# Row maxima of attention logits: two heads in the two halves of TensorE's rows instead of one head at a time

## Chip, cores and metric

The kernel runs on one core of a Trainium2 chip. The metric is the device time of one execution in microseconds (us). The core's engines are TensorE (PE in the profile; its weight loads are PEld), VectorE (DVE), ScalarE (ACT), GpSimd (POOL) and SyncE (SP), which here only issues transfers. Each engine works through its own instructions in order and waits on semaphores that others raise.

## The reference

One layer of a streaming encoder over 4096 tokens of width 1024. The part that matters is the sparse attention with 8 query heads of 64 in two groups, each group sharing one key and value head:

```python
iscore = jnp.where(allowed[None], iscore, -jnp.inf)
_, idx = lax.top_k(iscore, k_sel)                 # 256 keys for each query
...
s = jnp.einsum('bqgrd,bqkgd->bqgrk', qg, kg).astype(jnp.float32) * scale
s = jnp.where(valid[:, :, None, None, :], s, -jnp.inf)
p = jax.nn.softmax(s, axis=-1).astype(v.dtype)
o = jnp.einsum('bqgrk,bqkgd->bqgrd', p, vg)
```

Around it stand an RMS norm, the input projection, the index scores that choose the keys, a pooling branch, gates and the output projection. A softmax doesn't change when the same number is taken off all logits of a row, so the maximum that is subtracted may be a rough one.

## The kernel before

The kernel has four stages in a row: projection, index scores with the choice of keys, attention, output. Attention is the one that the change touches. It is dense: all keys up to the query's block are used, and a bias of 0 or -1e30 from the choice of keys takes out the others.

Queries are cut into 32 blocks `b` of 128. A unit is one block and one group `g` of four heads, so there are 64 units, and a unit of block `b` has `b + 1` tiles of 128 keys (1056 in all). For precision every number is held as a high part and a low part. `kk` holds the high part of the keys in rows 0 to 63 and again in rows 64 to 127, `kl` the low part in rows 0 to 63; `qa` holds the high parts of the queries in rows 0 to 63 and their low parts in rows 64 to 127, `qm` the high parts in rows 0 to 63 and, in row 64, the row's maximum.

For each unit:
- `maxima` (L1263): for each of the four heads, and for each chunk of up to 1024 keys, TensorE multiplies the head's 128 queries in `qa` with `kk` (L1280, up to two matmuls of 512 columns) into a tile `ps` of two banks, of which there are two. VectorE adds the bias and takes the maximum in one instruction (L1286), and at the end one maximum over the chunks (L1292). The maxima go through memory (`maxD`) into row 64 of `qm`.
- `softmax` (L1299): for each key tile TensorE makes the logits of four heads, keys in rows and queries in columns, with two matmuls (L1319, L1320) into one of three tiles `st` of one bank; VectorE adds the turned bias `bT` (L1323) into `tt`; ScalarE takes the exponential (L1326); GpSimd adds the exponentials up in `acc` (L1350, two key tiles at once); TensorE multiplies them with the values into `pv` (L1335), for up to four key tiles in one go, two heads into the lower 64 output partitions and two into the upper 64, each with 64 columns of weights. At the end the sums over keys are taken with a matmul (L1371), in the same split of columns.
- `queries` (L1217) turns the queries of a block by TensorE transposes (L341) through `st`, and ScalarE copies them into `qa` and `qm` (L1245, L1246).

The order of each engine's instructions is not that of the code. `Plan` (L120) plays all steps through with a cost in us, a due time (`key`) and tiles that must be free, and records them as they start: at each moment a free engine takes the step with the earliest key whose inputs are there and whose tiles are free. A change of `form` between two steps of an engine adds `CHF` (0.12) to the cost. What the chip does with that fixed order is another matter.

Of the kernel before, what the change touches and what calls it, by code (L numbers as in the profile page):

```python
# [12 lines left out]
F32 = mybir.dt.float32  # L13
F32R = mybir.dt.float32r
# [52 lines left out]
WOK = 45.0  # L67
WOD = 0.0
PVN = 4
IVL = 12.0  # L70
DU = 4
RB = 2
# [47 lines left out]
class Plan:  # L120
# [11 lines left out]
    def new(self, name):  # L132
        return Tile_(name)
# [113 lines left out]
class K:  # L247
# [893 lines left out]
    def phase_attention(self):  # L1141
# [26 lines left out]
        esr = ExitStack()  # L1168
        rp = esr.enter_context(tc.tile_pool(name="br", reuse_waits="tile", bufs=1, side="right"))
        shapes = {"k4": (K4, [P, 2, 2, 192], F32R), "q2": (2, [P, 8, P], F32R), "bias": (BB, [P, S], BF),  # L1170
                  "jk": (JK, [P, 1024], BF), "qa": (QB, [P, 8, P], F32R), "qm": (QB, [65, 8, P], F32R),
                  "bT": (2, [P, NB, P], BF), "mx": (4, [P, 4, 4], F32), "mf": (4, [P, 4], F32),
                  "tt": (TB, [P, 2, 4, P], F32), "acc": (2, [P, 2, 4, P], F32), "ov": (OV, [P, 2, P], F32),
                  "sm": (1, [P, 2, P], F32), "rl": (2, [P, 32], F32)}
        last = {"qa": (NB - 1) % QB, "qm": (NB - 1) % QB, "bT": (NB - 1) % 2}
        early = ("k4", "q2", "bias", "jk", "mf", "mx")
        banks = {"st": (SB, [P, 4, P], F32), "ps": (2, [P, 1024], F32), "pv": (1, [P, 2, P], F32)}
        pl = Plan()
        new = pl.new
        for pool, rings in ((sp, shapes), (pp, banks)):  # L1180
# [36 lines left out]
        def queries(b, base):  # L1217

            rows = slice(b * P, (b + 1) * P)
            L = P * (b + 1)  # L1220
            bias, q2, qa, qm = new("bias"), new("q2"), new("qa"), new("qm")
            ld = pl.add("dma", 0.8, base - 8, lambda: sp_dma(
                q2.t.rearrange("p h c -> p (h c)").bitcast(F32), self.hlD[rows, H_Q:H_K]), use=[q2])

            def load_bias():
                if b < 2:
                    gp.memset(bias.t[:, :L], 0.0)
                    gp.memset(bias.t[0:64, L - 64:L], -1e30)
                else:
                    sp_dma(bias.t[:, :L], self.biasD[b, :, :L])  # L1230
            lb = pl.add("pool" if b < 2 else "dma", 0.3 if b < 2 else 0.8, base - 8, load_bias, last_lb, use=[bias])
            last_lb[:] = [lb]
            done = []
            for f in range(2):
                pt = new("st")
                key = base + 2 + f
                sl = slice(f * 4, f * 4 + 4)

                def turn(pt=pt, f=f):
                    for h in range(4):  # L1240
                        self.turn(pt.t[:, h], q2.t[:, 4 * f + h])
                t = pl.add("pe", 0.24, key, turn, [ld], use=[pt, q2, qa, qm])

                def put(pt=pt, sl=sl):
                    act.activation(qa.t[:, sl], pt.t, AF.Copy)  # L1245
                    act.activation(qm.t[0:64, sl], pt.t[0:64], AF.Copy)  # L1246
                done.append(pl.add("act", 1.0, key, put, [t], use=[pt, qa, qm]))
            BI[b], Q[b] = (bias, lb), (qa, qm, done)

        def flip(b):  # L1250

# [11 lines left out]
        def maxima(u):  # L1263
# [4 lines left out]
            base, span = (at[u - 1], at[u] - at[u - 1]) if u else (-1, 1)  # L1268
            mx, mf = new("mx"), new("mf")
            last = None  # L1270
            for j in range(4):
                for c in range(n_c):
                    o, n = c * 1024, min(1024, L - c * 1024)
                    key = base + span * (j * L + o) / (4 * L) - AL
                    ps = new("ps")

                    def mm(ps=ps, o=o, n=n, j=j):
                        for s in range(0, n, 512):
                            e = min(n, s + 512)
                            pe.matmul(ps.t[:, s:e], Q[b][0].t[:, 4 * g + j], kk[:, g, o + s:o + e], start=True, stop=True)  # L1280
                    m = pl.add("pe", 0.44e-3 * n, key, mm, Q[b][2] + [K_[k] for k in range(o // P, (o + n) // P)], [ps],
                               [Q[b][0]])
                    jk = new("jk")

                    def reduce(ps=ps, jk=jk, o=o, n=n, c=c, j=j):
                        v.tensor_tensor_reduce(out=jk.t[:, :n], in0=ps.t[:, :n], in1=BI[b][0].t[:, o:o + n], scale=1.0,  # L1286
                                               scalar=-3e38, op0=OP.add, op1=OP.max, accum_out=mx.t[:, j, c:c + 1])
                    first = last is None
                    last = pl.add("dve", 0.075 + 1.04e-3 * n, key, reduce, [m, last, BI[b][1]],
                                  [jk] + ([mx] if first else []), [ps, BI[b][0]] + ([] if first else [mx]))  # L1290
            key = at[u] - AL + 0.5
            last = pl.add("dve", 0.12, key, lambda: v.tensor_reduce(  # L1292
                out=mf.t, in_=mx.t[:, :, 0:n_c], op=OP.max, axis=AX.X), [last], [mf], [mx])
# [5 lines left out]
        def softmax(u):  # L1299
            b, g = units[u]  # L1300
            hs = slice(4 * g, 4 * g + 4)
            qa, qm, _ = Q[b]
            bt, turned = BT[b]
            acc, pv, prev, pvs, T, E, done = new("acc"), new("pv"), None, None, {}, {}, 0
            direct = DIR if u == len(units) - 1 else 0
# [127 lines left out]
        for i in range(2):  # L1433
# [1 line left out]
            s0 = pl.add("dma", 1.0, E0 - 45, lambda g=g, i=i: sp_dma(  # L1435
                g.t, self.gD[8 + 2 * i:10 + 2 * i, :, 0:w2].rearrange("k p c -> p k c")), [s], use=[g])
            for m in (2 * i, 2 * i + 1):
                ps = new("ps")

                def mm(ps=ps, m=m):  # L1440
                    ms = slice(m * P, (m + 1) * P)
                    for k in range(4):
                        for x, y in ((0, 0), (0, 1), (1, 0)):
                            pe.matmul(ps.t[:, :w2], self.wb.get(x, k, ms), xs[k // 2][y].t[:, k % 2],
                                      start=(k == x == y == 0), stop=(k == 3 and x == 1))
# [199 lines left out]
```

## Time and profile before

| | us |
|---|---|
| runs of the kernel | 4258.36, 4262.97, 4265.87; median 4262.97 |
| the profiled execution | 4264.02, span 4262.3 |
| TensorE busy in the span (matmuls) | 4137.7 (97%) |
| VectorE, ScalarE, GpSimd busy | 3217.1 (75%), 2344.9 (55%), 1903.4 (45%) |

The busy shares are means over four stages. The rows of the section below are from views of the same execution: busy time by stretch, who waited for whom, a timeline of single engines (rows of the same line that follow each other are merged, with their count), and groups of instructions by line. In a timeline a row's second number is the time from the start of its first instruction to the end of its last. Matmuls are pipelined: the next begins while the one before has not ended, so the step from start to start is what one costs.

### The profile page before, as it was taken

To read this page: it belongs to the slowest core of one execution; us is meant where nothing else is said; L and a number is where in the kernel's file an instruction comes from. 1 tells how busy PE (TensorE), PEld (TensorE's weight loads), DVE (VectorE), ACT (ScalarE), POOL (GpSimd) and SP (SyncE) were. 2 spreads that over 40 slices of the span, in tenths; PEclk is the share of its full clock that TensorE was granted. 3 is DMA by queue.
4 is the path that set the end of the run, shared out by engine and by line. 5 is a ranking of instruction groups with operands and counts; after the bars stand their busy time and mean duration, and the time that the engine had idled before them with its cause. 6 is when DMAs were issued, how large, how long until landed. Compare 5 with 4: busy or idle time off the path is not lost.

```text
span 4262.3 us, 76690 instructions
## 1 busy us (share of the span) xinstructions
PE 4137.7 (97%) x27746; PEld 3492.4 (82%) x27747; DVE 3217.1 (75%) x7786; ACT 2344.9 (55%) x3977; POOL 1903.4 (45%) x1717
## 2 busy tenths in 40 slices
PE   8999899999999999999799999999999999999999
PEld 7988799899999998999756666666666658999998
DVE  5554688889899888788679999999999995434342
ACT  5444588767877877887455555555555552111110
POOL 3455222323234333010047888888999991111110
PEclk9999999999999999999899999999999999999999
DMA  6666644545444446565543212212111016544442
GB/s 227 242 239 233 208 156 169 176 172 184 166 174 164 163 168 196 204 233 200 190 85 72 57 45 49 48 47 52 42 41 39 23 42 190 163 134 151 137 144 77
DMA packets 442041, 586.32 MB, mean 138 GB/s; under 512 B 148861, under 2 KB 337849, under 8 KB 437434
## 3 DMA queue, kind: packets, MB, share of 16 engines
q1 hardware_dynamic: 441658, 581.39, 42.0%
q8 instruction: 219, 3.59, 0.3%
q14 instruction: 164, 1.34, 0.1%
HBM read 388.54 MB, written 175.54 MB: 132 GB/s over the span
## 4 chain that ended last, share of the span: by engine, by line
PE 47%; DVE 1%; DMA 1%; POOL 1%; issue 0%; ACT 0%; SPq 0%; DVEq 0%; POOLq 0%; ACTq 0%
PE pv L1335 11%; PE st L1319 7%; PE ps L1280 6%; PE st L1320 6%; PE po L1533 3%; PE po L1534 3%; PE po L1535 3%; PE pa L1534 3%; PE pa L1535 3%; PE pa L1533 3%; PE st L1371 1%; PE st L341 1%; POOL acc L1350 0%; DVE tt L1323 0%; DMA maxD<-mf 0%
## 5 line engine op out<-in xcount | busy, mean ns | idle before, releaser
L1052 PE MATMUL pd<-h,wgh 128*128 128x256 f32 x3584 | 1017.7, 284 | 1.3 <-DVE zsm L972 1.3
L1053 PE MATMUL pd<-h,wgh 128*128 128x256 f32 x3584 | 1011.1, 282 | 0.0
L1054 PE MATMUL pd<-h,wgl 128*128 128x256 f32 x3584 | 1010.5, 282 | 0.0
L1350 POOL TENSOR_TENSOR acc<-acc,tt 128x1024 f32<-128x1024 f32 x388 | 928.6, 2393 | 100.4 <-ACT tt L1326 77.4
L1326 ACT ACTIVATE tt<-tt 128x512 f32<-128x512 f32 x1056 | 653.7, 632 | 554.6 <-DVE tt L1323 552.7
L1323 DVE TENSOR_TENSOR tt<-st,bT 128x512 f32<-128x512 f32 x1056 | 694.4, 686 | 74.9 <-PE st L1320 57.8
L770 DVE SCALAR_TENSOR_TENSOR ring<-rl,wi,ring 128x1024 f32<-128x1024 f32 (+7 forms) x624 | 692.1, 1153 | 12.9 <-ACT rl L768 10.3
L1052 PEld LDWEIGHTS pd<-h,wgh 128*128 128x128 f32 x3584 | 679.7, 190 | 19.7 <-issue 1.5
L1053 PEld LDWEIGHTS pd<-h,wgh 128*128 128x128 f32 x3584 | 680.4, 190 | 14.7
L1286 DVE CUSTOM_DVE_ANT_0 jk<-ps,bias 128x1024 bf16<-128x1024 f32 (+7 forms) x640 | 657.2, 1030 | 44.3 <-PE ps L1280 34.4
L1054 PEld LDWEIGHTS pd<-h,wgl 128*128 128x128 f32 x3584 | 680.3, 190 | 0.0
L768 ACT ACTIVATE rl<-ps 128x1024 f32<-128x1024 f32 (+7 forms) x624 | 539.5, 890 | 134.5 <-PE ps L765 61.9
L1335 PE MATMUL pv<-tt,vv 128*64 128x256 f32 x4224 | 525.2, 389 | 0.0
L855 ACT ACTIVATE sg<-ring,tk 128x2048 fp8e4<-128x2048 f32 (+7 forms) x322 | 486.0, 1511 | 37.8 <-DVE tk L842 21.7
L1319 PE MATMUL st<-qa,kk 128*128 128x512 f32 x1056 | 452.1, 428 | 9.7 <-DVE tt L1323 5.5
L1335 PEld LDWEIGHTS pv<-tt,vv 128*64 128x64 f32 x4224 | 279.6, 137 | 210.7 <-issue 72.4
L1320 PE MATMUL st<-qm,kl 65*128 65x512 f32 x1056 | 419.9, 398 | 3.5 <-DMA qm<-maxD 3.5
L1575 POOL TENSOR_TENSOR ga<-ga,gb 128x256 f32<-128x256 f32 x128 | 100.8, 797 | 618.7 <-DVE ga L1570 507.3
L1280 PE MATMUL ps<-kk,qa 128*128 128x512 f32 (+3 forms) x1152 | 361.9, 390 | 0.7 <-DVE mx L1286 0.7
L765 PE MATMUL ps<-kis,qT 128*128 128x512 f32 (+3 forms) x1136 | 336.3, 383 | 14.4 <-ACT rl L768 14.3
L1498 ACT ACTIVATE yh<-ga 128x256 fp32r<-128x256 f32 x128 | 53.5, 419 | 501.7 <-PE po L1534 297.5
L1319 PEld LDWEIGHTS st<-qa,kk 128*128 128x128 f32 x1056 | 199.8, 189 | 151.4 <-DVE tt L1323 47.5
(329 smaller groups left out, 7792.5 us busy)
## 6 DMA issues: line engine op xcount, KB each, us to landing
h<-hD SPq DMA_DIRECT2D x192, 1024.0 KB
hlD<-rhl SPq DMA_DIRECT2D x32, 1280.0 KB
gD<-sgm SPq DMA_DIRECT2D x256, 128.0 KB
x<-x SPq DMA_DIRECT2D x32, 512.0 KB
wraw<-w_in SPq DMA_DIRECT2D x32, 512.0 KB
hD<-hh SPq DMA_DIRECT2D x32, 512.0 KB
hD<-hl SPq DMA_DIRECT2D x32, 512.0 KB
q<-hlD SPq DMA_DIRECT2D x32, 512.0 KB
```

The costliest lines, as they stand in the source:

```text
L770: prev[o] = pl.add("dve", 0.1 + n * 1.04e-3, k_, lambda rl=rl, o=o, n=n, h=h: v.scalar_tensor_tensor(acc[:, o:o + n], rl.t[:, :n], self.wi ...
L1052: pe.matmul(out, wh.t[:, k], r1, start=(k == 0), stop=False)
L1053: pe.matmul(out, wh.t[:, k], r2, start=False, stop=False)
L1054: pe.matmul(out, wl.t[:, k], r1, start=False, stop=(k == KT - 1))
L1280: pe.matmul(ps.t[:, s:e], Q[b][0].t[:, 4 * g + j], kk[:, g, o + s:o + e], start=True, stop=True)
L1286: v.tensor_tensor_reduce(out=jk.t[:, :n], in0=ps.t[:, :n], in1=BI[b][0].t[:, o:o + n], scale=1.0, scalar=-3e38, op0=OP.add, op1=OP.max, ac ...
L1319: pe.matmul(s.t, kk[:, g, o], qa.t[:, hs], start=True, stop=False)
L1320: pe.matmul(s.t, kl[:, g, o], qm.t[:, hs], start=False, stop=True)
L1323: ad = pl.add("dve", 0.602, i, lambda s=s, tt=tt, r=r, kt=kt: v.tensor_tensor(tt.t[:, r], s.t, bc(bt.t[:, kt:kt + 1], [P, 4, P]), op=OP.ad ...
L1326: E[kt] = pl.add("act", 0.52, i, lambda tt=tt, r=r: act.activation(tt.t[:, r], tt.t[:, r], AF.Exp), [ad], use=[tt])
L1335: pe.matmul(pv.t[64 * f:64 * f + 64], vv[:, k, 64 * g:64 * g + 64], T[k // 2].t[:, k % 2, 2 * f:2 * f + 2], start=(k == 0), stop=(k == b))
L1350: gp.tensor_tensor(acc.t, first, tt.t, op=OP.add)
```

## The change

The maxima are made for two heads at a time, from the high parts alone (before: high and low part of the query times the high part of the key). The even head's high parts are there already, in rows 0 to 63 of `qm`. For the odd head a new tile `qo` holds them in rows 64 to 127: for each block four more transposes of shifted columns (low part of the even head, high part of the odd one) into an `st` tile, of which ScalarE copies the lower half of the rows. A pair of matmuls uses 64 rows each, `kk` rows 0 to 63 and 64 to 127, which both hold the key's high part, and writes two tiles, `p0` and `p1`. Each has two banks, and there is one of each (before: two `ps` of two banks). One step of the plan makes both tiles (`form=2`), and the reductions of the two heads follow as two steps. The last stage's first four products, which used `ps`, take `p0` and `p1` in turn.

```diff
-                  "jk": (JK, [P, 1024], BF), "qa": (QB, [P, 8, P], F32R), "qm": (QB, [65, 8, P], F32R),
+                  "jk": (JK, [P, 1024], BF), "qa": (QB, [P, 8, P], F32R), "qm": (QB, [65, 8, P], F32R), "qo": (QB, [P, 4, P], F32R),
...
-        banks = {"st": (SB, [P, 4, P], F32), "ps": (2, [P, 1024], F32), "pv": (1, [P, 2, P], F32)}
+        banks = {"st": (SB, [P, 4, P], F32), "p0": (1, [P, 1024], F32), "p1": (1, [P, 1024], F32), "pv": (1, [P, 2, P], F32)}
...
-            BI[b], Q[b] = (bias, lb), (qa, qm, done)
+
+            pt = new("st")
+
+            def odd(pt=pt):
+                q = q2.t.rearrange("p h c -> p (h c)")
+                for i in range(4):
+                    self.turn(pt.t[:, i], q[:, 256 * i + 64:256 * i + 192])
+            t = pl.add("pe", 0.24, base + 4, odd, [ld], use=[pt, q2, qo])
+            done.append(pl.add("act", 0.5, base + 4, lambda: act.activation(qo.t[64:], pt.t[64:], AF.Copy), [t],
+                               use=[pt, qo]))
+            BI[b], Q[b] = (bias, lb), (qa, qm, done, qo)
...
-            for j in range(4):
+            qm, ready, qo = Q[b][1:]
+            for i in range(2):
                 for c in range(n_c):
                     o, n = c * 1024, min(1024, L - c * 1024)
-                    key = base + span * (j * L + o) / (4 * L) - AL
-                    ps = new("ps")
-
-                    def mm(ps=ps, o=o, n=n, j=j):
+                    key = base + span * (i * L + o) / (2 * L) - AL
+                    two = new("p0"), new("p1")
+
+                    def mm(two=two, o=o, n=n, i=i):
                         for s in range(0, n, 512):
                             e = min(n, s + 512)
-                            pe.matmul(ps.t[:, s:e], Q[b][0].t[:, 4 * g + j], kk[:, g, o + s:o + e], start=True, stop=True)
-                    m = pl.add("pe", 0.44e-3 * n, key, mm, Q[b][2] + [K_[k] for k in range(o // P, (o + n) // P)], [ps],
-                               [Q[b][0]])
+                            for f, (ps, q) in enumerate(zip(two, (qm.t[0:64, 4 * g + 2 * i], qo.t[64:, 2 * g + i]))):
+                                pe.matmul(ps.t[:, s:e], q, kk[64 * f:64 * f + 64, g, o + s:o + e], start=True, stop=True)
+                    m = pl.add("pe", 0.46e-3 * n, key, mm, ready + [K_[k] for k in range(o // P, (o + n) // P)], two,
+                               [qm, qo], form=2)
```

The reductions keep their code, once for each of the two tiles. Since the plan is played through again, the order around them moves. Two places show it.

TensorE in the middle of the attention stage, before: the maxima of a head stand between logits, as matmuls of the whole array like these.

```order
L1319 MATMUL st0_32377<-qa0_31846,kk_28394 128x512
L1320 MATMUL st0_32377<-qm0_31847,kl_28395 128x512
L1280 MATMUL ps1_32381<-kk_28394,qa1_32260 128x512 x2
L1319 MATMUL st1_32389<-qa0_31846,kk_28394 128x512
L1320 MATMUL st1_32389<-qm0_31847,kl_28395 128x512
L1335 MATMUL pv0_32392<-tt0_32311,vv_28396 64x256 x4
L1335 MATMUL pv0_32392<-tt1_32334,vv_28396 64x256 x4
L1319 MATMUL st2_32409<-qa0_31846,kk_28394 128x512
L1320 MATMUL st2_32409<-qm0_31847,kl_28395 128x512
```

The same engine in the same stage of the changed kernel, where the maxima are L1293, the logits L1333 and L1334 (`p00` and `p10` are the tiles `p0` and `p1`).

```order
L1334 MATMUL st1_31266<-qm0_30847,kl_28395 128x512
L1293 MATMUL p00_31272<-kk_28394,qm0_30847 128x512
L1293 MATMUL p10_31273<-kk_28394,qo0_30896 128x512
L1293 MATMUL p00_31272<-kk_28394,qm0_30847 128x128
L1293 MATMUL p10_31273<-kk_28394,qo0_30896 128x128
L1333 MATMUL st2_31283<-qa0_30846,kk_28394 128x512
L1334 MATMUL st2_31283<-qm0_30847,kl_28395 128x512
L1333 MATMUL st0_31289<-qa0_30846,kk_28394 128x512
L1334 MATMUL st0_31289<-qm0_30847,kl_28395 128x512
```

The maxima of two heads now stand in one island, half the rows each, and there are fewer, larger islands; more logits follow each other between them.

VectorE in the middle of the stage, before: each reduction (L1286, with a second instruction that reads its result out) stands alone between additions (L1323).

```order
L1323 TENSOR_TENSOR tt3_36321<-st2_36293,bT1_35669 128x512
L1286 ISA jk1_36334,mx3_36111<-ps1_36315,bias1_35301 128x1024
L1286 ISA mx3_36111 128x1
L1323 TENSOR_TENSOR tt3_36321<-st1_36337,bT1_35669 128x512
L1323 TENSOR_TENSOR tt4_36356<-st0_36348,bT1_35669 128x512
L1286 ISA jk0_36362,mx3_36111<-ps0_36353,bias1_35301 128x1024
L1286 ISA mx3_36111 128x1
L1323 TENSOR_TENSOR tt4_36356<-st1_36358,bT1_35669 128x512
```

The same engine in the changed kernel, where the reductions are L1300 and the additions L1337.

```order
L1337 TENSOR_TENSOR tt4_35892<-st0_35859,bT0_35289 128x512
L1337 TENSOR_TENSOR tt4_35892<-st2_35884,bT0_35289 128x512
L1300 ISA jk0_35913,mx1_35733<-p00_35874,bias0_34904 128x1024
L1300 ISA mx1_35733 128x1
L1300 ISA jk1_35932,mx1_35733<-p10_35875,bias0_34904 128x1024
L1300 ISA mx1_35733 128x1
L1337 TENSOR_TENSOR tt0_35937<-st1_35908,bT0_35289 128x512
L1337 TENSOR_TENSOR tt0_35937<-st0_35939,bT0_35289 128x512
L1337 TENSOR_TENSOR tt3_35962<-st1_35952,bT0_35289 128x512
L1300 ISA jk0_35968,mx1_35733<-p00_35956,bias0_34904 128x896
```

The two reductions of a pair stand behind each other, and the additions that stood between single reductions are gathered between pairs.

## Rows read from the trace of the kernel before

**Rows 1.** Busy time of each engine by stretch of the attention stage (first the stretch's length).

```profile
core 0: us, PE busy (x) PEld busy (x) DVE busy (x) ACT busy (x) POOL busy (x), PEclk, DMA share, GB/s
2117.00:2200.00 83.00, 73.31 (x378) 48.09 (x377) 56.05 (x155) 43.69 (x93) 23.96 (x18) 0.81 0.52 108
2200.00:3400.00 1200.00, 1199.37 (x7051) 793.01 (x7051) 1125.41 (x2097) 659.98 (x1166) 1047.98 (x474) 1.00 0.21 48
3400.00:3520.00 120.00, 113.85 (x634) 70.35 (x632) 110.18 (x167) 65.65 (x112) 112.75 (x49) 0.96 0.14 39
```

**Rows 2.** Waits of TensorE's matmuls, 2200 to 3400: us in total, times, longest.

```profile
PE st L1371 <- POOL acc L1361: 0.6, 2, 0.3
```

**Rows 3.** Waits of VectorE, 2200 to 3400: the two longest.

```profile
DVE tt L1323 <- PE st L1320: 41.3, 85, 1.7
DVE jk L1286 <- PE ps L1280: 23.4, 44, 1.8
```

**Rows 4.** Timeline of TensorE: start, us, line, tiles, shapes, count.

```profile
2701.43 0.40 PE L1319 MATMUL st<-qa,kk 128*128 128x512 f32 x1
2701.66 0.40 PE L1320 MATMUL st<-qm,kl 65*128 65x512 f32 x1
2701.90 0.64 PE L1280 MATMUL ps<-kk,qa 128*128 128x512 f32 x2
2702.47 1.95 PE L1335 MATMUL pv<-tt,vv 128*64 128x256 f32 x16
2704.34 0.50 PE L1319 MATMUL st<-qa,kk 128*128 128x512 f32 x1
2704.68 0.40 PE L1320 MATMUL st<-qm,kl 65*128 65x512 f32 x1
```

**Rows 5.** The same, cut to windows from 2702.4 and from 2702.7.

```profile
2702.47 0.44 PE L1335 MATMUL pv<-tt,vv 128*64 128x256 f32 x2
...
2702.47 0.65 PE L1335 MATMUL pv<-tt,vv 128*64 128x256 f32 x4
```

**Rows 6.** Timeline of TensorE in the projection stage.

```profile
106.80 0.28 PE L349 MATMUL ma<-wkvh,hl 128*128 128x256 f32 x1
106.92 0.60 PE L393 MATMUL pt<-ident,x 128*128 128x128 f32 x4
107.28 0.38 PE L347 MATMUL mb<-wih,hh 128*128 128x296 f32 x1
107.50 0.30 PE L348 MATMUL mb<-wil,hh 128*128 128x296 f32 x1
```

**Rows 7.** Timeline of VectorE.

```profile
2702.76 1.28 DVE L1323 TENSOR_TENSOR tt<-st,bT 128x512 f32<-128x512 f32 x2
2703.96 1.22 DVE L1286 CUSTOM_DVE_ANT_0 jk<-ps,bias 128x1024 bf16<-128x1024 f32 x1
2705.09 0.09 DVE L1286 DVE_READ_ACCUMULATOR2_ANT mx<- 128x1 f32 x1
2705.12 0.69 DVE L1323 TENSOR_TENSOR tt<-st,bT 128x512 f32<-128x512 f32 x1
```

**Rows 8.** Groups by line: GpSimd's additions (busy us, mean ns, idle before).

```profile
L1350 POOL TENSOR_TENSOR acc<-acc,tt 128x1024 f32<-128x1024 f32 x388 | 928.6, 2393 | 100.4 <-ACT tt L1326 77.4 <-POOL acc L1350 0.5
```

**Rows 9.** Groups by line and shape: the matmuls of the maxima.

```profile
L1280 PE MATMUL ps<-kk,qa 128*128 128x512 f32 x960 | 320.2, 405 | 0.0
L1280 PE MATMUL ps<-kk,qa 128*128 128x384 f32 x64 | 23.4, 375 | 0.0
L1280 PE MATMUL ps<-kk,qa 128*128 128x256 f32 x64 | 19.6, 315 | 0.2 <-DVE mx L1286 0.2
L1280 PE MATMUL ps<-kk,qa 128*128 128x128 f32 x64 | 15.5, 255 | 0.5 <-DVE mx L1286 0.5
```

**Rows 10.** Timeline of TensorE: one batch of transposes.

```profile
2716.61 0.49 PE L341 MATMUL st<-identr,q 128*128 128x128 f32 x4
```

**Rows 11.** Groups by line: ScalarE's copies of half the rows.

```profile
L1246 ACT ACTIVATE qm<-st 64x512 fp32r<-64x512 f32 x64 | 37.5, 586 | 0.0
```

More of the change, by code (lines that the diff above doesn't have):

```diff
@@ L69 @@
 PVN = 4
+MPE = 0
 IVL = 12.0
@@ L1175, in phase_attention @@
         last = {"qa": (NB - 1) % QB, "qm": (NB - 1) % QB, "bT": (NB - 1) % 2}
-        early = ("k4", "q2", "bias", "jk", "mf", "mx")
-        banks = {"st": (SB, [P, 4, P], F32), "ps": (2, [P, 1024], F32), "pv": (1, [P, 2, P], F32)}
+        early = ("k4", "q2", "bias", "jk", "mf", "mx", "qo")
+        banks = {"st": (SB, [P, 4, P], F32), "p0": (1, [P, 1024], F32), "p1": (1, [P, 1024], F32), "pv": (1, [P, 2, P], F32)}
         pl = Plan()
@@ L1220, in queries @@
             L = P * (b + 1)
-            bias, q2, qa, qm = new("bias"), new("q2"), new("qa"), new("qm")
+            bias, q2, qa, qm, qo = new("bias"), new("q2"), new("qa"), new("qm"), new("qo")
             ld = pl.add("dma", 0.8, base - 8, lambda: sp_dma(
@@ L1278, in mm @@
                         for s in range(0, n, 512):
                             e = min(n, s + 512)
-                            pe.matmul(ps.t[:, s:e], Q[b][0].t[:, 4 * g + j], kk[:, g, o + s:o + e], start=True, stop=True)
-                    m = pl.add("pe", 0.44e-3 * n, key, mm, Q[b][2] + [K_[k] for k in range(o // P, (o + n) // P)], [ps],
-                               [Q[b][0]])
[L1283 to L1287, printed above, removed]
@@ L1288, in maxima @@
-                    first = last is None
-                    last = pl.add("dve", 0.075 + 1.04e-3 * n, key, reduce, [m, last, BI[b][1]],
-                                  [jk] + ([mx] if first else []), [ps, BI[b][0]] + ([] if first else [mx]))
+                            for f, (ps, q) in enumerate(zip(two, (qm.t[0:64, 4 * g + 2 * i], qo.t[64:, 2 * g + i]))):
+                                pe.matmul(ps.t[:, s:e], q, kk[64 * f:64 * f + 64, g, o + s:o + e], start=True, stop=True)
+                    m = pl.add("pe", 0.46e-3 * n, key, mm, ready + [K_[k] for k in range(o // P, (o + n) // P)], two,
+                               [qm, qo], form=2)
@@ new lines, in maxima, with reduce @@
+                    for j, ps in enumerate(two):
+                        jk = new("jk")
+                        def reduce(ps=ps, jk=jk, o=o, n=n, c=c, j=2 * i + j):
+                            v.tensor_tensor_reduce(out=jk.t[:, :n], in0=ps.t[:, :n], in1=BI[b][0].t[:, o:o + n], scale=1.0,
+                                                   scalar=-3e38, op0=OP.add, op1=OP.max, accum_out=mx.t[:, j, c:c + 1])
+                        first = last is None
+                        last = pl.add("dve", 0.075 + 1.04e-3 * n, key, reduce, [m, last, BI[b][1]],
+                                      [jk] + ([mx] if first else []), [ps, BI[b][0]] + ([] if first else [mx]))
@@ L1301, in softmax @@
             hs = slice(4 * g, 4 * g + 4)
-            qa, qm, _ = Q[b]
+            qa, qm, _, _ = Q[b]
             bt, turned = BT[b]
@@ L1437, in phase_attention @@
             for m in (2 * i, 2 * i + 1):
-                ps = new("ps")
+                ps = new(f"p{m % 2}")
                 def mm(ps=ps, m=m):
```

## The prediction

> **What bounds the kernel now.** I read the busy times by stretch first. The change touches only the attention stage, from about 2117 to 3520 us, some 1403 us of the profiled execution's 4264.0 us (span 4262.3). In its middle 1200 us TensorE is busy for 1199.4, VectorE for 1125.4, GpSimd for 1048.0 and ScalarE for 660.0, at a granted clock of 1.00 [rows 1]. The reader should not stop at the 1199: matmuls overlap, so busy is not full. The list of waits settles it: over those 1200 us TensorE's matmuls waited 0.6 us for anybody [rows 2], while VectorE stood 41.3 us waiting for logits (L1320) and 23.4 us for maxima (L1280) [rows 3]. So TensorE sets the pace; VectorE follows with 74.6 us of idle time (1200 - 1125.4), and that is the most a faster TensorE can win here before VectorE is the bound.
>
> Third, the timeline of TensorE, for the price of one instruction. Matmuls of 512 columns follow each other every 0.23 us (2701.43, 2701.66, 2701.90; I use 0.232) [rows 4]. The value products (L1335, 64 output columns each) run two at a time: two of them fit into 0.44 us [rows 5], and sixteen take 1.95 us, 0.38 of it the last one's own length, so a pair of records goes every 0.22 us (0.217 over the last six steps) [rows 4].
>
> The same rows price something less visible, the change between the whole array and the array split in two. From the second maxima matmul (2701.90 + 0.64 - 0.40 = 2702.14) to the first value product it is 0.33 instead of 0.23: 0.10 lost; the first step inside the group costs 0.05 more than the others (four records in 0.65, so 0.27 against 0.22). On the way back, from the last value product (2704.04) to the logits at 2704.34, 0.30 instead of 0.22: 0.09 by these rounded starts, and I use 0.10; and from that first matmul to the next 0.34 instead of 0.23: 0.11, the weights that could not be loaded ahead. That is 0.15 into the split array and 0.21 out of it. The type of the operands is not what costs: in the projection stage four fp32 transposes between fp32r products cost nothing beyond their own steps (106.80 to 107.50 is 0.70 for one step of 0.12, four of 0.11 and one of 0.14, 0.70) [rows 6].
>
> VectorE's prices: two additions (L1323) start 1.20 apart from what follows, 0.60 each; a reduction over 1024 columns takes 1.16 (2703.96 to 2705.12) [rows 7]. GpSimd's addition of two key tiles is 2.39 [rows 8]. So for four key tiles of one unit before: TensorE 8 x 0.232 logits + 4 x 0.232 maxima + 8 x 0.217 values + 0.36 mode changes = 4.88; VectorE 4 x 0.60 + 2 x 1.16 = 4.72; GpSimd 2 x 2.39 = 4.79. Three engines within 4%. That is the main thing to see.
>
> **The change, part by part.**
> *Streaming saved.* The maxima have 960 matmuls of 512 columns and 64 each of 384, 256 and 128 [rows 9]. If the two halves of the rows run side by side, as the two halves of the columns do in [rows 5], half of them costs nothing: 480 x 0.232 = 111.4, and 32 x (384 + 256 + 128) columns at 0.232/512 us each = 11.1. Together 122.5 us. No row shows two row halves at work, so the price of a pair lies between 0.232 (side by side) and 0.464 (one after the other), a saving of 122.5 or 0. I take the former, by the nearest row.
>
> *Mode changes added.* Every pair step is now an island of split rows. Counted in TensorE's order of instructions, there were 309 changes into the column-split mode and 309 out. Now it is 177 from the whole array to split rows, 142 from split columns to split rows, 288 from split rows to whole, 31 from split rows to split columns, 186 from split columns to whole, 297 from whole to split columns: 1121 against 618. Priced like the column split [rows 4]: before 309 x (0.15 + 0.21) = 111. After: into columns 328 x 0.15 = 49; into rows 319 x 0.21 = 67 (0.10, and 0.11 since 128 weight columns have to be loaded, as on the way back); out to whole 474 x 0.21 = 100. That is 216, so 105 us are added. No row shows the row mode, so the bound on the other side is that it needs no change at all: then what remains is 328 x 0.15 and as many ways out at 0.21, 118, some 7 added. I take the column price: it is the nearest row and [rows 6] leaves the mode as its cause.
>
> The rows give this price for split columns only. The Trainium skill (TensorEngine Tiling (Array Packing), "Key Properties") says that changing the tiling mode, and not only the tile, drains the engine; it names no price and makes no difference between splits of rows and of columns. By that rule the 105 us stand; without it the first rival below comes true.
>
> *Odd heads.* 32 more batches of four transposes, a step of 0.08 each after the first (0.49 for four, 0.25 the last one's length) [rows 10], so about 0.33 a batch: 10 us. 32 more ScalarE copies of half the rows at 0.59 [rows 11], 19 us, beside an engine that is busy for 55% of the stretch. They hold one of the three logits tiles meanwhile; if that were never hidden, the 19 us would be the price; at best 0. I take 2.
>
> *Reductions and waits.* The 640 reductions keep their sizes. What moves is their order: in 285 of the 320 pairs the two now stand right behind each other in VectorE's order, and 3 or 4 additions stand ahead of the next pair in 230 pairs, 2 or fewer in 85. Before, two additions stood ahead of most reductions (394 of 640). The second matmul of a pair waits for the second tile's reduction, and behind it on TensorE's queue the logits and value products. Over four key tiles VectorE does 2.32 us of reductions, frees no logits tile meanwhile, then does 2.40 us of additions. In those 2.32 TensorE has three free logits tiles (3 x 0.46 = 1.4) and a value group (about 2.0); in the additions' 2.40 it has the pair (0.10 + 0.34 + 0.40 until its result, under 1.0). So with 3 or 4 additions both sides are covered, and I put the new wait at 0 for these. For the rest see the third rival. GpSimd gets the same instructions in the same order, and SP's queue the same DMAs, some a few places earlier or later.
>
> The sum: -122.5 + 105 + 10 + 2 = about -6 us on an engine that waits for nobody. By cycles: four key tiles with a pair beside a value group now cost TensorE 4.88 - 0.46 + 0.21 = 4.63, with a pair alone among logits 4.88 - 0.46 + 0.42 = 4.84. In the first kind VectorE's 4.72 takes over, which costs some of the gain, but the slack then hides some of the turns and sums. I leave the sum as it is: 4264.0 - 6 = 4258 for that execution, which lies 1.0 above the median of the runs (4262.97). So 4257.
>
> **The rivals.**
> *Split rows change mode cheaply.* TensorE loses 122.5 and gains 7 + 12: about -103, more than VectorE's 64.7 us of waits for TensorE in the middle [rows 3]. VectorE then bounds, GpSimd at 1048 of 1200 close behind. Of the 65 some 45 to 60 come: about 4211. For it: only the column split is on record. Against: the 0.10 to drain and the 0.11 to load have nothing that belongs to columns alone.
>
> *The pair of single tiles becomes the wait* (slower). Before, two tiles alternated: one head could be written while the other was reduced. Now a pair must be wholly reduced before the next is wholly written. The place is the second matmul of the pair. The 85 pairs with two additions or fewer ahead cover at most 1.2 us, and a value group of 2.0 us can stand in the way. If one pair in five (64) finds its tile unreduced and TensorE waits 0.8 us each, that is 51 us, with the sum's -6 together 45: 4308; for half as many pairs it is 4282. It decides from the point where TensorE's waits for VectorE exceed some 15 us in the middle stretch. For it: three engines within 4%, and [rows 3] shows VectorE already starved now and then. Against: today's TensorE waits 0.6 us in all [rows 2], so there is no hint of such handoffs failing.
>
> *The halves don't run side by side* (the change doesn't do what it says). Then 122.5 come back and nothing hides them: about 4380. Against: [rows 5].
>
> **How the numbers follow.** Forecast 0.46, its own range 4242 to 4276; cheap mode change 0.20; pair handoff 0.25; no concurrency 0.09. What a measurement tells from no change is 0.2%, 8.5 us, so faster means under 4254.4 and slower over 4271.5. The forecast lies 6 us below the median and spreads by some 12: 0.42 of it faster, 0.46 same, 0.12 slower. Faster: 0.19 + 0.20 = 0.39; same: 0.21 + 0.02 of the handoff's mild end = 0.23; slower: 0.06 + 0.23 + 0.09 = 0.38. The range has to reach both to the cheap change and to the full handoff: 4208 to 4312; the last rival is left out.
>
> **What would show it.** Right: pairs of records of the new line starting together every 0.23 us; 0.33 from a logits matmul to the first of them and 0.30 back, with 0.34 behind each; TensorE's waits for VectorE still a few us in the middle; VectorE's idle time about as now. Cheap change: 0.23 at both edges, and VectorE over 97% busy. Handoff: tens of us on TensorE behind reductions of the new line. No concurrency: 0.23 between the two halves. The forecast falls if the stage gets shorter than 1365 us or longer than 1420.

## The result, and the profile after

| | median us (runs) | against the kernel before, 95% interval |
|---|---|---|
| before | 4261.9 (4258.36 to 4265.87) | |
| after | 4287.2 (4285.42 to 4294.94) | 1.0062 [1.005, 1.0075] |

The change makes the kernel 25 us slower. The forecast was 4257, 6 us faster; the time lies inside the range that was given with it, in the second rival's interval ("The pair of single tiles becomes the wait", 4282 to 4308).

The page of the profiled execution (4288.47 us) gives busy time, share of the span and instructions of each engine:

```profile
span 4286.7 us, 76875 instructions
PE 4147.6 (97%) x27874; PEld 3375.8 (79%) x27875; DVE 3219.2 (75%) x7786; ACT 2350.6 (55%) x4009; POOL 1899.8 (44%) x1717
```

The shares are means over four stages and don't show where the time went. The same three stretches as in [rows 1], of the kernel after:

```profile
2117.00:2200.00 83.00, 72.64 (x389) 42.43 (x389) 53.39 (x148) 43.84 (x95) 20.60 (x14) 0.77 0.47 100
2200.00:3400.00 1200.00, 1184.39 (x7024) 672.88 (x7025) 1106.39 (x2064) 654.30 (x1173) 1026.12 (x468) 0.99 0.21 48
3400.00:3520.00 120.00, 114.66 (x665) 64.64 (x663) 111.51 (x178) 64.74 (x111) 111.88 (x49) 0.99 0.09 24
```

In the middle 1200 us TensorE now stands for 15.6 us (1200 - 1184.4; before 0.6), and VectorE for 93.6 instead of 74.6, so both engines idle more. What TensorE's matmuls waited for there (us in total, times, longest), against the 0.6 of [rows 2]:

```profile
PE p L1293 <- DVE mx L1300: 6.7, 15, 0.8
PE st L342 <- ACT qm L1247: 1.2, 2, 0.6
PE st L1385 <- POOL acc L1375: 1.1, 2, 0.6
```

And VectorE, against the 41.3 and 23.4 of [rows 3]:

```profile
DVE tt L1337 <- PE st L1334: 47.5, 85, 2.2
DVE jk L1300 <- PE p L1293: 41.3, 56, 3.4
```

The maxima wait for reductions, and the reductions wait 18 us longer for maxima: a handoff that misses in both directions. The timeline of TensorE of the kernel after (columns as in [rows 4]) shows a pair among logits:

```profile
2704.80 0.40 PE L1334 MATMUL st<-qm,kl 65*128 65x512 f32 x1
2705.14 0.50 PE L1293 MATMUL p<-kk,qm 64*128 64x512 f32 x1
2705.14 0.49 PE L1293 MATMUL p<-kk,qo 64*128 64x512 f32 x1
2705.47 0.39 PE L1293 MATMUL p<-kk,qm 64*128 64x512 f32 x1
2705.47 0.39 PE L1293 MATMUL p<-kk,qo 64*128 64x512 f32 x1
2705.80 0.50 PE L1333 MATMUL st<-qa,kk 128*128 128x512 f32 x1
2706.14 0.40 PE L1334 MATMUL st<-qm,kl 65*128 65x512 f32 x1
```

The two heads' matmuls start in the same hundredth of a microsecond: the halves of the rows do run side by side. The edges cost about what the column split cost in [rows 4]: 0.34 from the logits to the pair, 0.33 from the first pair to the second, 0.33 back to the logits and 0.34 behind them, where 0.23 is the plain step. That is some 0.42 for one island of two pairs, as priced. Here the Trainium skill (TensorEngine Tiling (Array Packing), "Key Properties": a change of the tiling mode drains the engine) and the trace agree, for rows as for columns.

That a pair costs no more than one matmul is seen against an island with a single pair, here from the row split with two tiles for each head (below):

```profile
2800.43 0.49 PE L1293 MATMUL p<-kk,qm 64*128 64x512 f32 x1
2800.44 0.49 PE L1293 MATMUL p<-kk,qo 64*128 64x512 f32 x1
2800.86 0.49 PE L1333 MATMUL st<-qa,kk 128*128 128x512 f32 x1
2801.19 0.39 PE L1334 MATMUL st<-qm,kl 65*128 65x512 f32 x1
```

From the pair to the logits it is 0.43; with two pairs it was 0.33 + 0.33, so the second pair adds 0.23, the plain step.

VectorE in the same moment of the kernel after: a pair's two reductions stand behind each other, then three additions.

```profile
2705.92 1.22 DVE L1300 CUSTOM_DVE_ANT_0 jk<-p,bias 128x1024 bf16<-128x1024 f32 x1
2707.06 0.08 DVE L1300 DVE_READ_ACCUMULATOR2_ANT mx<- 128x1 f32 x1
2707.06 1.22 DVE L1300 CUSTOM_DVE_ANT_0 jk<-p,bias 128x1024 bf16<-128x1024 f32 x1
2708.20 0.08 DVE L1300 DVE_READ_ACCUMULATOR2_ANT mx<- 128x1 f32 x1
2708.20 1.88 DVE L1337 TENSOR_TENSOR tt<-st,bT 128x512 f32<-128x512 f32 x3
```

Where the time went is seen by adding up TensorE's steps from start to start over the stage, by the kind of matmul that begins a step. From the start of the first maxima matmul to that of the last sums matmul the stage is 1415.0 us before and 1440.4 after, +25.4, the whole difference. The steps that begin with maxima fell by 66.3 (280.1 to 213.9). Those that begin with logits rose by 66.6 (L1319 to L1333: 285.0 to 316.6; L1320 to L1334: 272.9 to 307.9); mode changes and waits are both in it. Those that begin with transposes rose by 19.2 (32.3 to 51.5), those with value products by 3.7. Steps over 0.36 us were 78 and are 167; their excess over 0.34 rose from 25.2 to 53.2 us. The loss is spread over many small steps, and no list of waits names all of it.

### The profile page after: what moved, and what is told of

Read it like the earlier page. It is cut to its first block, busy times and chain, and to the rows that moved or that the text cites. A ratio compares the mean times of both kernels' runs of the same rounds, so it can differ in the third digit from the quotient of the medians.

```text
span 4286.7 us, 76875 instructions
## 1 busy us (share of the span) xinstructions
PE 4147.6 (97%) x27874; PEld 3375.8 (79%) x27875; DVE 3219.2 (75%) x7786; ACT 2350.6 (55%) x4009; POOL 1899.8 (44%) x1717
## 4 chain that ended last, share of the span: by engine, by line
PE 44%; DVE 3%; POOL 1%; DMA 1%; issue 1%; ACT 1%; SPq 0%; DVEq 0%; ACTq 0%; POOLq 0%
PE pv L1349 10%; PE st L1333 7%; PE st L1334 5%; PE p L1293 4%; PE po L1547 3%; PE po L1548 3%; PE po L1549 3%; PE pa L1548 3%; PE pa L1549 3%; PE pa L1547 3%; POOL acc L1364 1%; DVE jk L1300 1%; PE st L342 1%; PE st L1385 1%; DVE tt L1337 1%
## 5 line engine op out<-in xcount | busy, mean ns | idle before, releaser
L1340 ACT ACTIVATE tt<-tt 128x512 f32<-128x512 f32 x1056 | 641.8, 630 | 510.8 <-DVE tt L1337 506.8
L1337 DVE TENSOR_TENSOR tt<-st,bT 128x512 f32<-128x512 f32 x1056 | 675.4, 683 | 71.6 <-PE st L1334 68.2
L1300 DVE CUSTOM_DVE_ANT_0 jk<-p,bias 128x1024 bf16<-128x1024 f32 (+7 forms) x640 | 638.9, 1031 | 68.0 <-PE p L1293 67.5
L1333 PE MATMUL st<-qa,kk 128*128 128x512 f32 x1056 | 483.4, 458 | 15.3 <-DVE tt L1337 8.7
L1334 PE MATMUL st<-qm,kl 65*128 65x512 f32 x1056 | 422.6, 400 | 3.6 <-DMA qm<-maxD 3.6
L1333 PEld LDWEIGHTS st<-qa,kk 128*128 128x128 f32 x1056 | 199.9, 189 | 225.3 <-DVE tt L1337 100.0
L964 POOL COPY halo<-u 128x16 f32<-128x16 f32 x64 | 24.5, 382 | 606.3 <-ACT u L958 606.3
```

The costliest lines, as they stand in the source:

```text
L1333: pe.matmul(s.t, kk[:, g, o], qa.t[:, hs], start=True, stop=False)
L1334: pe.matmul(s.t, kl[:, g, o], qm.t[:, hs], start=False, stop=True)
L1337: ad = pl.add("dve", 0.602, i, lambda s=s, tt=tt, r=r, kt=kt: v.tensor_tensor(tt.t[:, r], s.t, bc(bt.t[:, kt:kt + 1], [P, 4, P]), op=OP.ad ...
L1340: E[kt] = pl.add("act", 0.52, i, lambda tt=tt, r=r: act.activation(tt.t[:, r], tt.t[:, r], AF.Exp), [ad], use=[tt])
```

## The experiments

Times of different groups of runs are compared by the ratio to the kernel before in the same group.

**Is it TensorE's own work or the handoff?** Two kernels with half the reducing work: the reductions leave out the second half of each row's columns, and the exponent is scaled so that it stays finite.

```diff
-  v.tensor_tensor_reduce(out=jk.t[:, :n], in0=ps.t[:, :n], in1=BI[b][0].t[:, o:o + n], ...
+  v.tensor_tensor_reduce(out=jk.t[:, :n // 2], in0=ps.t[:, :n // 2], in1=BI[b][0].t[:, o:o + n // 2], ...
-  act.activation(tt.t[:, r], tt.t[:, r], AF.Exp)
+  act.activation(tt.t[:, r], tt.t[:, r], AF.Exp, scale=0.01)
```

> The kernel before, but each reduction of the maxima reads only the first half of its columns, and the exponent is scaled by 0.01 so that it stays finite; the order of instructions is that of before. VectorE loses some 280 us of work. Theory H (handoff: the change made TensorE's own work a few us shorter, as summed, and what was lost are waits of TensorE that come from the pair of single tiles and VectorE's two reductions in a row): TensorE hardly waited in before, so 4252 to 4262 us. Theory W (own work: mode changes and transposes cost TensorE more than the sum says): the same, 4252 to 4262. It is the base line for the next run.

> The changed kernel with the same halved reductions and the same scaled exponent, in the changed kernel's order. With VectorE far from its bound, what is left is TensorE's own work. H: within 8 us of the run with halved reductions of before, so 4246 to 4264. W: 18 to 30 us above that run, 4272 to 4290, as without the halving.

Measured: before with it 0.9994 [0.9985, 1.0003], after with it 1.0001 [0.9992, 1.001]. The middle stretch of the first, then of the second (columns as in [rows 1]):

```profile
2200.00:3400.00 1200.00, 1199.43 (x7068) 797.39 (x7068) 886.12 (x2104) 661.00 (x1169) 1051.45 (x476) 1.00 0.21 48
```

```profile
2200.00:3400.00 1200.00, 1191.74 (x7162) 684.95 (x7161) 890.35 (x2102) 666.64 (x1195) 1046.79 (x476) 1.00 0.21 48
```

With VectorE freed of 216 us there (1106.4 to 890.4), the changed kernel gives back 22 to 26 of its 25 us. What is left, mode changes and odd transposes included, is +3 to +4 us (by the ratios; 4265.31 against 4260.96). That is an upper bound on TensorE's own work, where the sum said -6: in the second run TensorE still stands 8.3 us of the middle stretch (1200 - 1191.7), in the first 0.6. The rest hangs on VectorE's time; the runs below show by which handoff.

TensorE's granted clock is another candidate. In the kernel after it fell to the lower of its two levels (1.2 GHz) for short times in two windows of the middle stretch, in which TensorE stood 1.5 and 2.9 us; elsewhere in that stretch it was 1.00:

```profile
2200.00:2300.00 100.00, 98.52 (x591) 55.94 (x592) 86.26 (x183) 57.78 (x109) 71.62 (x38) 0.98 0.32 69
2550.00:2650.00 100.00, 97.13 (x553) 54.56 (x551) 86.77 (x170) 51.06 (x92) 80.75 (x37) 0.95 0.20 48
```

The same kernel with halved reductions has two such windows too:

```profile
2200.00:2300.00 100.00, 98.18 (x585) 55.47 (x585) 68.67 (x183) 57.95 (x109) 71.67 (x38) 0.98 0.33 69
3000.00:3100.00 100.00, 98.73 (x584) 57.16 (x579) 71.45 (x169) 53.73 (x96) 87.33 (x39) 0.97 0.20 48
```

By these rows the clock costs at most some 7 us in the one and 5 in the other (an estimate: 0.02 and 0.05, 0.02 and 0.03, of 100 us each). So it doesn't make the difference between them; and the pairs alone (below) lose more at a granted clock of 1.00.

**Does the grouping into pairs alone cost it?** The kernel before, with the two heads of a pair in one step and one tile for each, but whole-row matmuls from `qa` (so no odd heads):

```diff
-        banks = {..., "ps": (2, [P, 1024], F32), ...
+        banks = {..., "p0": (1, [P, 1024], F32), "p1": (1, [P, 1024], F32), ...
+                            for f, ps in enumerate(two):
+                                pe.matmul(ps.t[:, s:e], Q[b][0].t[:, 4 * g + 2 * i + f], kk[:, g, o + s:o + e], ...
-                    m = pl.add("pe", 0.44e-3 * n, key, mm, ..., [ps],
+                    m = pl.add("pe", 0.88e-3 * n, key, mm, ..., two,
```

> The kernel before with one part of the change: two heads are made in one step into two tiles of two banks, one of each, and then reduced; but with all 128 rows for each head, one after the other, so no split rows, no new mode changes and no odd heads' transposes. H: the handoff alone costs what the change lost and what it saved on top, 4280 to 4300. W: as before, 4260 to 4268.

Measured: 1.0086 [1.0072, 1.01], +36 us, with no row split at all. Its middle stretch, and two of its waits:

```profile
2200.00:3400.00 1200.00, 1184.19 (x6849) 764.26 (x6846) 1097.17 (x2042) 633.43 (x1136) 1013.35 (x461) 1.00 0.20 47
```

```profile
DVE jk L1288 <- PE p L1281: 50.8, 68, 2.9
DVE tt L1325 <- PE st L1322: 47.9, 78, 1.8
PE p L1281 <- DVE mx L1288: 7.3, 12, 0.8
```

It is the same picture as after: TensorE stands 15.8 us, and VectorE waits 50.8 us for maxima. Its order also has 659 mode changes against 615 by the same count.

**And the row split alone?** The order of the changed kernel, instruction for instruction, with whole-row matmuls:

```diff
-  for f, (ps, q) in enumerate(zip(two, (qm.t[0:64, 4 * g + 2 * i], qo.t[64:, 2 * g + i]))):
-      pe.matmul(ps.t[:, s:e], q, kk[64 * f:64 * f + 64, g, o + s:o + e], ...
+  for f, ps in enumerate(two):
+      pe.matmul(ps.t[:, s:e], Q[b][0].t[:, 4 * g + 2 * i + f], kk[:, g, o + s:o + e], ...
```

> The changed kernel in its own order, instruction for instruction, but each maxima matmul uses all 128 rows (high and low part, as before): no split of rows, so two heads' matmuls run one after the other. By the sum TensorE gains 122.5 us of streaming and loses 98 us of mode changes against the changed kernel, +24. H: some of that fills waits, so 4292 to 4312. W (mode changes dearer than 98 by 20 or more): 4287 or less.

Measured: 1.0133 [1.0117, 1.0148], 4320.82, above the 4312 expected. By the ratios the row split gives 30 us on this order (1.0133 to 1.0062), about the 24 of the expectation. Against the pairs alone (1.0086) this run is 20 us slower: it also has the odd heads' transposes and another order, and no run takes these two apart.

**Are the two reductions behind each other the trouble?** The second reduction of a pair gets a later due time, so additions come between:

```diff
-  last = pl.add("dve", 0.075 + 1.04e-3 * n, key, reduce, ...
+  last = pl.add("dve", 0.075 + 1.04e-3 * n, key + j * span * n / (4 * L), reduce, ...
```

> The changed kernel with one number of the plan changed: the second reduction of a pair gets its due time later by half the pair's share, so additions stand between the two reductions again (436 reductions stand alone, 92 pairs are left). The two tiles stay single. Theory L (lumps: two reductions in a row free no logits tile for 2.3 us, and TensorE's logits wait for that): most of the 22 us come back, 4264 to 4274. Theory S (single tiles: the pair waits for its own second tile, whatever the order): no better, 4282 or more, since the second tile now comes free later.

Measured: 1.0088 [1.0074, 1.0102], no better than after. TensorE's idle time in the middle rose to 28.2 us, and two waits are:

```profile
PE st L1333 <- DVE tt L1337: 15.7, 45, 0.8
DVE jk L1300 <- PE p L1293: 70.6, 124, 1.7
```

VectorE waits 70.6 us for maxima where it waited 41.3 in the kernel after: the next pair comes later still. That it does because the second reduction holds its tile longer is likely, not shown; TensorE itself now waits most for logits tiles.

**What do the odd heads cost?** After without the 32 batches of transposes and their copies (rows 64 to 127 of `qa` stand in for `qo`):

> The changed kernel without the odd heads' transposes and copies: the odd head's maxima are made from rows 64 to 127 of the tile that the logits use, which hold low parts, so these maxima are wrong; the exponent is scaled by 0.01 to stay finite. 128 transposes and 32 copies fewer. By the 12 us of the prediction 4275; by the steps after transposes in the trace of the changed kernel, 51.5 us against 32.3 before, 4264 to 4272; if waits fill what is taken away, 4280 to 4288.

Measured: 1.0046 [1.0032, 1.006], about 7 us less than after by the ratios, with intervals that overlap. In its trace the steps that begin with transposes take 40.8 us, 10.7 less than after and still 8.5 more than before. So of the 19.2 us above 10.7 are the odd heads' own steps, some 0.33 for each of the 32 batches; the rest is growth of transposes that both kernels have.

**Is it the second matmul of the pair?** The pair-only kernel with its matmuls ordered by head (both of the first head's, then both of the second's):

```diff
-  for s in range(0, n, 512):
-      e = min(n, s + 512)
-      for f, ps in enumerate(two):
+  for f, ps in enumerate(two):
+      for s in range(0, n, 512):
+          e = min(n, s + 512)
```

> The pair run with the matmuls inside a step in another order: both of the first head, then both of the second, so that only the third matmul waits for the second tile, and VectorE can begin the first reduction 0.46 us earlier. If the second matmul's wait is the place of the loss, some 10 to 20 of its 36 us come back: 4280 to 4291. If the loss is that the whole step stands behind both reductions in TensorE's order, 4295 to 4302.

Measured: 1.0078 [1.0064, 1.0092], as with the pair alone (1.0086). So the place is not the second matmul. The plan explains it: it starts a pair's step only when both tiles are free, so the whole step stands behind both reductions. The same kernel as the pair alone, with the halved reductions:

> The kernel before with the pair in one step (whole rows, two single tiles) and, as in the first run, reductions over half their columns and the scaled exponent; the order is that of the pair run, planned for whole reductions. S (TensorE waits until a pair's tiles are reduced): with reductions half as long the tiles come free in time, so of the 36 us of the pair run at most 12 are left, 4262 to 4276. If it is the order that brings the loss, whatever the reductions take: 4285 or more.

Measured: 1.0047 [1.0033, 1.0061], 17 us less and half of the 36 left, which neither theory had. VectorE's time counts, but light reductions alone don't free the pair: TensorE still stands 7.8 us of the middle stretch.

```profile
2200.00:3400.00 1200.00, 1192.24 (x6967) 780.20 (x6967) 879.43 (x2072) 643.62 (x1156) 1035.28 (x469) 1.00 0.21 48
```

**Single tiles, or long steps?** Pairs of 512 columns, so that the same four banks hold two tiles for each head. VectorE then has 1152 reductions instead of 640:

```diff
-        banks = {..., "p0": (1, [P, 1024], F32), "p1": (1, [P, 1024], F32), ...
+        banks = {..., "p0": (2, [P, 512], F32), "p1": (2, [P, 512], F32), ...
-            n_c = -(-L // 1024)
+            n_c = -(-L // 512)
```

> The same with whole reductions and the right exponent: 1152 reductions in place of 640, some 40 us more for VectorE, which has 75 us to spare in the middle of the kernel before. S: better than the pair run's 4300 in spite of that, 4270 to 4290. If VectorE or the order decides: 4298 or more.

> The pair in one step with whole rows, halved reductions and the scaled exponent, as the run at 4282, but with tiles of one bank, two for each head of the pair, and chunks of 512 columns: the same banks, and one pair can be written while the other is reduced. S (single tiles make the loss that is left): 4264 to 4274. If the order of a pair step makes it: 4280 or more.

Measured: 1.0009 [0.9999, 1.0018] with whole reductions, 0.9997 [0.9988, 1.0006] with halved ones. The last run leaves the steps at 512 columns and takes the second tile away:

```diff
-        banks = {..., "p0": (2, [P, 512], F32), "p1": (2, [P, 512], F32), ...
+        banks = {..., "p0": (1, [P, 512], F32), "p1": (1, [P, 512], F32), ...
```

> Against the kernel before. The run with pairs of 512 columns and two tiles for each head differed from the pair of 1024 columns in two things: a step half as long, and a second tile to write while the first is reduced. Here the step stays at 512 columns and the second tile is taken away (one bank for each head, two banks empty). If the single tiles are the cause, each pair again stands wholly behind both reductions of the pair before, twice as often: 36 us or more, 4300 to 4340. If the length of the step was the cause, the time stays by that run's: 4264 to 4272.

Measured: 4357.1, 1.021 [1.0193, 1.0227], +91 us, above the 4340 expected. The middle stretch with two tiles for each head, then with one:

```profile
2200.00:3400.00 1200.00, 1199.56 (x7037) 788.72 (x7036) 1151.23 (x3014) 657.57 (x1163) 1045.40 (x473) 1.00 0.21 48
```

```profile
2200.00:3400.00 1200.00, 1163.00 (x6572) 741.81 (x6571) 1090.75 (x2820) 613.27 (x1096) 967.38 (x440) 0.99 0.20 47
```

VectorE's wait for maxima, in the same two:

```profile
DVE jk L1288 <- PE p L1281: 4.5, 11, 1.0
```

```profile
DVE jk L1288 <- PE p L1281: 78.1, 117, 2.8
```

So the number of tiles decides: with two the pairs cost 4 us, hardly clear of nothing, though VectorE works most, and with one 91. How the 91 come about is not all told by the tiles themselves. TensorE's longest wait in the run with one tile, absent from its list with two, is

```profile
PE st L1322 <- DMA qm<-maxD: 22.7, 18, 3.2
```

These are logits that wait for the maxima on their way through memory into `qm`; for the pair's own tiles TensorE's matmuls wait 0.4 us there. Pairs that come late make the maxima late: that is the likely link, not a measured one. In the timelines of the run with one tile, VectorE's reductions of one pair:

```profile
2804.97 0.68 DVE L1288 CUSTOM_DVE_ANT_0 jk<-p,bias 128x512 bf16<-128x512 f32 x1
2805.58 0.08 DVE L1288 DVE_READ_ACCUMULATOR2_ANT mx<- 128x1 f32 x1
2805.58 0.69 DVE L1288 CUSTOM_DVE_ANT_0 jk<-p,bias 128x512 bf16<-128x512 f32 x1
2806.19 0.08 DVE L1288 DVE_READ_ACCUMULATOR2_ANT mx<- 128x1 f32 x1
```

and TensorE around them, with the sums' wait for VectorE in brackets:

```profile
2803.32 0.65 PE L1373 MATMUL st<-acc,ones 128*64 128x256 f32 x4 [0.31 <-DVE tt L1325]
2803.90 0.73 PE L1281 MATMUL p<-kk,qa 128*128 128x512 f32 x2
...
2806.05 1.95 PE L1337 MATMUL pv<-tt,vv 128*64 128x256 f32 x16
2807.93 0.50 PE L1281 MATMUL p<-kk,qa 128*128 128x512 f32 x1
```

A pair is written at 2803.90, read until 2806.19, and a value group that began at 2806.05 stands ahead of the next pair, which starts at 2807.93. A value group in the way is what the rival described; logits that wait for late maxima are not in it.

**Then the row split with two tiles?** After, with the same edit:

> The changed kernel (split rows, odd heads) with tiles of one bank, two for each head, and chunks of 512 columns, so that the handoff is gone as in the pair with two tiles each; but twice as many islands of split rows: 1605 mode changes in place of 615 before. By the prices of the prediction 320 into columns x 0.15, 552 into rows x 0.21 and 733 out to whole x 0.21 are 318 us against 111: +207, with -122.5 streaming and +19 transposes +104, so 4355 to 4375. If mode changes into and out of rows are cheaper than the column price, clearly less; if single tiles were the only loss, 4255 to 4270.

Measured: 1.0152 [1.0135, 1.0169], +65 where +104 was expected. The expectation had 19 us for the odd transposes (10.7 by the run without them) and 0.42 for each of 552 islands, where the median steps of this trace give 0.39 (0.33, 0.43 and 0.34, less three plain steps of 0.23 to 0.24); these two are 8 and some 17 of the 39 us, the rest is open. The middle stretch:

```profile
2200.00:3400.00 1200.00, 1198.76 (x6797) 649.75 (x6797) 1105.52 (x2870) 641.36 (x1139) 990.23 (x450) 1.00 0.20 48
```

TensorE stands 1.2 us, so the handoff is gone, but one pair to an island means 1605 mode changes. With four banks the split as tried here has either single tiles or twice the islands, and no version here beats the kernel before.

**Can the order be mended?** Six runs changed what the plan believes or prefers. After with `CHF` at 0.21 (before: 0.12):

> The changed kernel with the plan's cost of a mode change at the measured 0.21 in place of 0.12, so that its order is made with a truer TensorE: 1161 mode changes (more than 1116), 83 pairs right behind column-split work in place of 142. If the untrue cost made the order's waits, 4270 to 4280; if not, the additional mode changes show, 4287 to 4300.

Measured: 1.0037 [1.0023, 1.005], with 1161 mode changes. After with the plan's costs set to the trace's (`CHF` 0.18, transposes 0.33, exponential 0.60, GpSimd's addition 2.45, and some others by less):

> The changed kernel with the same true costs in its plan. If the handoff's 22 us come from an order made for a wrong machine, they mostly go: 4264 to 4273, next to the 4265 of the run with halved reductions. If they are in the single tiles, no better than the run with the true form cost: 4275 to 4288.

Measured: 1.0031 [1.0019, 1.0044]. The same costs in the kernel before:

> The kernel before with the plan's costs set to what the trace shows (mode change 0.18, logits 0.464, maxima 0.453 per 1000 columns, exponential 0.60, GpSimd's additions 2.45, reductions 0.09 + 1.045 per 1000, transposes 0.33). 583 mode changes in place of 615, so 6 us less of TensorE: 4254 to 4264.

Measured: 0.9999 [0.999, 1.0008]. So a better order takes back some 8 to 13 of the 25 us. After with a plan that takes a step in a split mode behind another one, within 4 units of due time (1050 mode changes, 1116 by the same count in after):

> The changed kernel with a plan that, after a step in one of the two split modes, takes another such step first if it is due within 4 units: 1050 mode changes in place of 1116. At 0.10 to 0.21 us each TensorE's own work falls by 7 to 14 us. If that decides, 4272 to 4281; if the handoff of single tiles decides, 4282 to 4295.

Measured: 1.0083 [1.0069, 1.0097], 9 us more than after and above both ranges: fewer mode changes did not pay. The kernel before with such a plan (531 mode changes against 615), and with value groups of up to six key tiles (`PVN` 6, 505 mode changes):

> The kernel before with a plan that stays in a mode while a step of that mode is due within 4 units: 531 mode changes in place of 615. At 0.15 in and 0.21 out, 84 of them are 15 us of TensorE, which waited for nobody: 4247 to 4256. If the order that it makes brings waits instead, 4262 or more.

> The kernel before with value groups of up to six key tiles in place of four: 505 mode changes in place of 615, so 110 x 0.18 = 20 us less of TensorE, which waits for nobody before. If nothing else moves, 4243 to 4252; if later value products hold tiles and make others wait, 4262 or more.

Measured: 0.9996 [0.9987, 1.0005] and 1.0029 [1.0017, 1.0041], where both were expected faster: misses. Fewer mode changes, in orders that moved with them, gained nothing. In the first of the two TensorE is busy for 69.1 us of the first stretch, before 73.3 [rows 1], so its order lost time at the start of the stage; how much of the expected 15 us that took is open.

## Why the prediction was wrong

- What bounds the kernel: right. TensorE set the pace before; 239 us less of VectorE's work in the middle stretch (1125.4 to 886.1) moved the time by 0.06%.
- Streaming saved, 122.5: right in kind. The pairs start together, and a second pair in an island adds 0.23, so the third rival (halves that run one after the other) falls.
- Mode changes, 0.15 into columns, 0.21 into rows and out: right in size at both edges (0.34, 0.33, 0.34 in the trace). The first rival (a cheap row mode) falls.
- Odd heads, 10 us: right as far as the steps show it (10.7), and the run without them is some 7 us shorter.
- The sum of these, -6: not refuted. The halved reductions leave +3 to +4, with 8.3 us of TensorE's idle time and a clock worth up to 5 us still in it.
- Reductions and waits: this is the step that failed, "I put the new wait at 0 for these". It asked whether the engines have enough other work over a cycle of four key tiles, and by averages they have. But, as the runs with one tile and with two show, what counts is when a tile comes free: each pair's step needs both tiles free, and both come free only after 2.3 us of reductions and whatever stands ahead of them in VectorE's fixed order; when the pair is late, VectorE runs out of both reductions and logits. The runs put 22 to 26 us in place of the 0 (after against after with halved reductions); 8 to 13 of them go with truer costs in the plan. The stage took 1440.4 us, past the 1420 at which the prediction itself gives its forecast up.
- The second rival named this mechanism and its price (TensorE's waits of 26 to 51 us); it had 0.25. That the range held the time is due to this rival alone. Its signs did not come: it asked for more than 15 us of TensorE's waits for VectorE in the middle stretch, and for tens of us behind the new reductions; the list has some 9, of which 6.7 behind the reductions, and the 15.6 us of idle time have all causes in them. Its place was wrong too: the whole step waits, not the second matmul, and the loss shows as VectorE's idle time and as many slightly longer steps. And the argument against it, that TensorE's 0.6 us of waits [rows 2] give no hint of failing handoffs, proved nothing: that figure belongs to two tiles that alternate, which the change takes away.

Not settled: why half of the pair's 36 us stay with halved reductions. TensorE's 7.8 us of idle time are part of it, and 44 more mode changes, 22 round trips at 0.36, may be 8 more (an estimate; with 84 fewer the kernel before gained nothing). Also open: how much of the loss lies in the order that the plan makes for single tiles and how much in its waits on the chip, since every count of tiles comes with an order of its own.

## What to carry to other kernels

Two tiles used in turn are a double buffer; writing both in one step makes them a single one of twice the size, and on three engines within 4% of each other that cost 36 us here, with the order that the plan made for it (91 with steps half as long). A small wait in the profile before is no evidence on a handoff whose buffers the change removes: count the buffers of each handoff, before and after, ahead of adding up instructions. When an array is split for a few matmuls at a time, count the islands: some 0.4 us of steps for one pair of heads ate most of a saving of 0.46 here.

## What was not expected of the hardware

Fewer changes of the array's mode did not make the kernel before faster: 531 instead of 615 gave 0.9996, though each round trip shows 0.36 us in the timeline. And with one tile of 512 columns for each head TensorE's longest wait was not for a tile but, 22.7 us of the middle stretch, for the maxima's way through memory.
